# A decoder layer that begins with x: two input blocks first, sums of squares on TensorE, S5 parameters on GpSimd, memory keys and values between the memory-query blocks

## The chip, the cores and the metric

The kernel runs on one core of one Trainium2 chip. The metric is device time in microseconds (us) of one execution. A core has TensorE (PE), which multiplies, VectorE (DVE), ScalarE (ACT) and GpSimd (POOL) for elementwise work, and SyncE (SP), which here issues all large DMAs. Each engine works through its own list of instructions strictly in order, and waits on semaphores for what others produce.

## The reference

One layer of a hybrid decoder trunk, for 512 prompt tokens and 8 sample tokens (520 columns in all). The start of the layer, cut to what the change touches:

```
h = rmsnorm(x, norm1_g)                       # x * rsqrt(mean(x*x) + EPS) * g
u, q, k, v, qm, gl = split(h @ w_in)          # u 512 wide, qm 512, q, k, v 768 each, gates 3072
b_ssm = glu(gelu(s5_scan(u, ...)))            # diagonal complex state space model
#   dt = exp(log_dt); mag = exp(a_re*dt); ab = mag*(cos(a_im*dt) + i sin(a_im*dt)); q = (ab - 1)/a; bb = q*b
#   s = scan over tokens of (ab*s + bb@u);  y = Re(c@s) + d*u
b_att = dilated windowed attention of q, k, v
mk, mv = split(rmsnorm(mem, mem_norm_g) @ w_mem_kv)   # 256 memory tokens
b_mem = softmax(qm @ mk.T) @ mv @ w_mem_o
x = x + (sum of sigmoid(gate_b) * branch_b) @ w_out
x = x + (gelu(conv(h2 @ w_up_a)) * (h2 @ w_up_v)) @ w_down
```

## The kernel before

Weights come in blocks of 128 x 1024 fp32 (512 KB), one SP DMA each (`wload`). For full precision each block is split into a rounded high part (ACT, line 163) and the remainder (DVE, the subtraction at line 80, called from `wload`). A product is three matmuls (lines 192, 193 and 195 in `dense`): high by high, low activations by high weights, high by low. An input block (u0 to u3, qm0 to qm3, k0 to k5, q, v) is 8 row chunks by 2 halves of 260 columns by 3 products, 48 matmuls. `wahead(4)` keeps four blocks loading ahead. Dense results lie in two PSUM slots (`ps_dense`), small ones in four (`ps_small`); block n can begin only when the result of block n-2 has been evacuated.

RMSNorm is applied late: the raw products are multiplied by the reciprocal root of each token at evacuation (`rstd`; `mrs` and `mrt` for the memory). `rms_stat` sums the squares over partitions with a matmul against ones, makes the root by Newton steps on DVE (tiles `xr_*`, `mr_*`), and `rms_bcast` spreads it with diagonal matrices (`xr_dg`) and matmuls into `ps_xb`, copied to `rstd` (line 248).

The program begins with the memory: memT, then keys (mk0 to mk3, 24 matmuls of 256 columns each) and values (mv0 to mv3, 12 matmuls of 512 columns each), then u0 to u3, qm, k, q, v, the gates. The squares of x and memory are made by ACT and added on GpSimd (`xacc`, `macc`).

The S5 branch: `s5_params` (tiles `s5t`, on DVE) makes powers of the decay and a rotation (`rotc`, `rots`) out of a small DMA (line 382), with polynomials in place of exp and sin; `s5_rot` doubles that rotation into tables `rc` (GpSimd) and `rsn` (DVE); `s5_start` opens tables (`gr`, `gi`, `gt`) and four batches (`s5_batches`), which are coroutines fed between the matmuls of the blocks. A scheduler sets each engine's order from emission and priority: `urgent()` raises a piece by PRIO, and `s5_params` is lowered by LOWP; the order is then fixed in the program.

Of the kernel before, what the change touches and what calls it, by code (L numbers as in the profile page):

```python
# [15 lines left out]
OP = mybir.AluOpType  # L16
# [24 lines left out]
POOLW = ("in1",)  # L41
# [5 lines left out]
def order(*names):  # L47
# [3 lines left out]
FIRST = order("u0", "u1", "u2", "u3", "qm0", "qm1", "qm2", "qm3", "k0", "k1", "k2", "k3", "k4", "k5",  # L51
              "q0", "q1", "q2", "q3", "q4", "q5")
# [4 lines left out]
TD0, TD1, TD2, TD3, TD4 = 18, 8, 4, 9, 8  # L57
# [3 lines left out]
def build(nc, tc, I, O):  # L61
# [53 lines left out]
    def weights():  # L115
        for f in range(4):
            yield f"mk{f}", I["wmk"][f]
        for c in range(4):
            yield f"mv{c}", I["wmv"][c]
        for i in [IN0[n] + f for n, f in FIRST] + list(range(20, 26)):  # L120
            yield f"in{i}", I["wi"][i]
# [26 lines left out]

    def wload():
# [68 lines left out]
    def rms_stat_(pt, accs, n, name, pl):  # L218
# [7 lines left out]
        V.tensor_scalar(ms_, pt[:, :nb], 1.0 / D, EPS, OP.mult, OP.add)  # L226
# [63 lines left out]
    mv = mp.tile([P, 2, 512], F32, name="mv")  # L290
    ms_cm, ms = pool("memstage", 1, side="right")
# [39 lines left out]
    def s5_params():  # L331
# [7 lines left out]
        def ts(a, s1, op0, s2=None, op1=None):  # L339
            o = tn(a.shape)  # L340
            if op1 is None:
                V.tensor_scalar(o, a, s1, None, op0)
            else:
                V.tensor_scalar(o, a, s1, s2, op0, op1)
            return o

        def t2(a, b, op):
            o = tn(a.shape)
            tt(V, o, a, b, op)
            return o  # L350
# [118 lines left out]

    def mem_squares():  # L470
        tt(G, macc, memT[:, 0], memT[:, 0], OP.mult)
        for k in range(1, KB):
            msq = ms.tile([P, NMEM], F32, tag=f"xsq{k % 2}", name=f"msq{k}")
            A.activation(msq, memT[:, k], AF.Square)
            tt(G, macc, macc, msq, OP.add)

    def x_part(k):
        S.dma_start(xt[:, k:k + 2], I["xT"][:, k:k + 2])
        for i in (k, k + 1):
            split(xh[:, i], xl[:, i], xt[:, i], gv[:, 0, i:i + 1])  # L480
            if i == 0:
                A.activation(xacc, xt[:, i], AF.Square)
            else:
                sq = ms.tile([P, NT], F32, tag=f"xsq{i % 2}", name=f"xsq{i}")
                A.activation(sq, xt[:, i], AF.Square)
                tt(G, xacc, xacc, sq, OP.add)

    pmk = []
    for f in range(4):
# [1080 lines left out]
```

## Time and profile before

| | |
|---|---|
| median of 3 runs | 988.45 us (987.79 to 993.16) |
| the profiled execution | 990.76 us |
| its span | 989.0 us |
| PE busy | 947.1 us, 96% of the span |
| DVE, ACT, POOL busy | 554.0, 299.6, 192.6 us |

The span is the time between the first and the last recorded instruction; the 1.8 us beside it are start and end of the launch. The profiled execution was 2.3 us above the median. PE is busy nearly everywhere, so the time is what PE has to do plus the places where it stands still or runs at a lower clock.

### The profile page before, as it was taken

The numbers are of one execution on the slowest core, as the hardware profiler recorded it, in microseconds if no ns is written. First come the engines' busy times: TensorE is split into PE (matmuls) and PEld (weight loads), VectorE is DVE, ScalarE is ACT, GpSimd is POOL, SyncE is SP. The second block draws the span as 40 slices with busy tenths as digits, with TensorE's granted clock in tenths as the row PEclk, the third lists the DMA queues.
The fourth block names the chain that finished last, engine by engine and source line by source line (L and its number), as shares of the span: only waits on it lengthen the run. The fifth ranks groups of instructions, "written<-read, shape, count | busy, mean of one in ns | idle before, by whom it ended". The sixth has DMA issues, their size and how long they took to land.

```text
span 989.0 us, 19819 instructions
## 1 busy us (share of the span) xinstructions
PE 947.1 (96%) x8373; PEld 914.1 (92%) x8373; DVE 554.0 (56%) x1017; ACT 299.6 (30%) x480; POOL 192.6 (19%) x261
## 2 busy tenths in 40 slices
PE   8798899989999999999999999999999999999996
PEld 7597899877999998999999999999999999999995
DVE  6999976445455434344655676555555555423234
ACT  6412232224354322123323233322323322222220
POOL 4359542012003301100210350000000000012110
PEclk9998999989999999999999999999999999999998
DMA  7543335531322127563322532223223223332312
GB/s 236 188 152 107 92 104 192 149 95 65 133 87 75 44 68 243 195 229 116 96 91 92 162 118 95 86 93 100 86 86 106 88 85 97 91 99 80 97 39 87
DMA packets 47305, 112.36 MB, mean 114 GB/s; under 512 B 13600, under 2 KB 21408, under 8 KB 45600
## 3 DMA queue, kind: packets, MB, share of 16 engines
q1 hardware_dynamic: 47216, 111.09, 35.0%
q8 instruction: 66, 1.08, 0.4%
q14 instruction: 23, 0.19, 0.1%
HBM read 101.36 MB, written 9.71 MB: 112 GB/s over the span
## 4 chain that ended last, share of the span: by engine, by line
PE 58%; DVE 1%; POOL 1%; ACT 0%; issue 0%; DVEq 0%; ACTq 0%; POOLq 0%
PE ps_y L192 4%; PE ps_y L195 4%; PE ps_y L193 4%; PE ps_uv L195 4%; PE ps_uv L192 4%; PE ps_uv L193 4%; PE ps_ua L192 4%; PE ps_ua L195 4%; PE ps_ua L193 4%; PE ps_g L192 3%; PE ps_g L195 3%; PE ps_g L193 3%; PE ps_x L195 2%; PE ps_x L192 2%; PE ps_x L193 2%; PE ps_me L193 1%
## 5 line engine op out<-in xcount | busy, mean ns | idle before, releaser
L192 PE MATMUL ps_g<-xh,wh_in 128*128 128x260 f32 x384 | 102.0, 287 | 0.0
L193 PE MATMUL ps_g<-xl,wh_in 128*128 128x260 f32 x384 | 99.9, 282 | 0.0
L192 PE MATMUL ps_y<-gh,wh_dn 128*128 128x260 f32 x352 | 93.0, 283 | 0.0
L193 PE MATMUL ps_y<-gl,wh_dn 128*128 128x260 f32 x352 | 93.0, 283 | 0.0
L192 PE MATMUL ps_uv<-hh,wh_uv 128*128 128x260 f32 x352 | 91.9, 282 | 0.0
L192 PE MATMUL ps_ua<-hh,wh_ua 128*128 128x260 f32 x352 | 91.8, 282 | 0.0
L193 PE MATMUL ps_uv<-hl,wh_uv 128*128 128x260 f32 x352 | 91.6, 282 | 0.0
L193 PE MATMUL ps_ua<-hl,wh_ua 128*128 128x260 f32 x352 | 91.6, 282 | 0.0
L163 ACT CAST wh_in<-wr_in 128x1024 fp32r<-128x1024 f32 x50 | 52.3, 1051 | 106.4 <-PE ps_g L193 35.8
L195 PE MATMUL ps_g<-xh,wl_in 128*128 128x260 f32 x384 | 77.2, 283 | 0.0
L192 PEld LDWEIGHTS ps_g<-xh,wh_in 128*128 128x128 f32 x384 | 72.3, 188 | 2.6 <-issue 2.4
L195 PE MATMUL ps_y<-gh,wl_dn 128*128 128x260 f32 x352 | 74.4, 282 | 0.0
L80 DVE TENSOR_TENSOR wl_in<-wr_in,wh_in 128x1024 fp32r<-128x1024 f32 x49 | 67.5, 1378 | 8.8 <-ACT wh_in L163 7.2
L193 PEld LDWEIGHTS ps_g<-xl,wh_in 128*128 128x128 f32 x384 | 72.2, 188 | 0.0
L195 PE MATMUL ps_uv<-hh,wl_uv 128*128 128x260 f32 x352 | 71.2, 283 | 0.0
L195 PE MATMUL ps_ua<-hh,wl_ua 128*128 128x260 f32 x352 | 70.9, 283 | 0.0
L192 PEld LDWEIGHTS ps_uv<-hh,wh_uv 128*128 128x128 f32 x352 | 66.4, 189 | 0.0
L192 PEld LDWEIGHTS ps_ua<-hh,wh_ua 128*128 128x128 f32 x352 | 66.3, 188 | 0.0
L193 PEld LDWEIGHTS ps_y<-gl,wh_dn 128*128 128x128 f32 x352 | 66.2, 188 | 0.0
L192 PEld LDWEIGHTS ps_y<-gh,wh_dn 128*128 128x128 f32 x352 | 66.2, 188 | 0.0
L193 PEld LDWEIGHTS ps_uv<-hl,wh_uv 128*128 128x128 f32 x352 | 66.1, 188 | 0.0
L193 PEld LDWEIGHTS ps_ua<-hl,wh_ua 128*128 128x128 f32 x352 | 66.1, 188 | 0.0
(440 smaller groups left out, 2497.5 us busy)
## 6 DMA issues: line engine op xcount, KB each, us to landing
wr_in<-in_wi SPq DMA_DIRECT2D x50, 512.0 KB, 3.4
wr_ua<-in_wup SPq DMA_DIRECT2D x22, 512.0 KB, 3.3
wr_uv<-in_wup SPq DMA_DIRECT2D x22, 512.0 KB, 3.3
wr_dn<-in_wdn SPq DMA_DIRECT2D x16, 448.0 KB, 3.3
wr_glu<-in_wglu SPq DMA_DIRECT2D x8, 512.0 KB, 3.2
mkc<-in_smk SPq DMA_DIRECT2D x4, 1024.0 KB, 6.4
mvc<-in_smv SPq DMA_DIRECT2D x4, 1024.0 KB, 6.2
wr_out<-in_wout SPq DMA_DIRECT2D x8, 512.0 KB, 3.2
```

The source lines that it names most:

```text
L80: e.tensor_tensor(o, a, b, op)
L163: A.copy(hi[:, a:b], raw[:, a:b])
L192: T.matmul(ps[:, a:b], lhsT=wh, rhs=ah[:, t0:t1], start=st, stop=False)
L193: T.matmul(ps[:, a:b], lhsT=wh, rhs=al[:, t0:t1], start=False, stop=False)
L195: T.matmul(ps[:, a:b], lhsT=wl, rhs=ah[:, t0:t1], start=False, stop=en)
```

## The change

- x and the input blocks u0 and u1 are loaded first, in pieces (`wload_begin`, `x_part`), and u0 and u1 are computed together, chunk by chunk. Their raw products are copied by ACT to `spare[1]` (storage of kT that is not in use yet). Memory follows.
- The sums of squares are made on PE: ACT writes the squares to `spare`, and matmuls with 32 columns of ones add them (`square_sums`), 16 for x, 8 for the memory; `rms_stat` divides by 32 copies.
- `s5_params` runs on GpSimd. What was one scalar-tensor-tensor instruction on DVE becomes a TENSOR_SCALAR and a TENSOR_TENSOR (`t3`, `horner`). `s5_rot` and `s5_decay` are emitted right behind the evacuations of u, with temporaries in kT.
- The memory blocks go between the qm blocks: mk0, mk1 after qm1, mk2, mk3 after qm2, mv0 to mv3 after qm3. `s5_start` comes after mv3.
- `s5_batches` sends the state part of batch n+1 ahead of the output part of batch n, with `ug`, `fr`, `fi` in two buffers.

The diff at its core ("..." marks what is left out):

```diff
-FIRST = order("u0", "u1", "u2", "u3", "qm0", "qm1", "qm2", "qm3", "k0", "k1", "k2", "k3", "k4", "k5",
-              "q0", "q1", "q2", "q3", "q4", "q5")
+FIRST = order("u0", "u1", "u2", "u3", "qm0", "qm1", "mk0", "mk1", "qm2", "mk2", "mk3", "qm3", "mv0", "mv1", "mv2",
+              "mv3", "k0", "k1", "k2", "k3", "k4", "k5", "q0", "q1", "q2", "q3", "q4", "q5")
...
+    def wload_begin(name, src):
+        raw = wp.tile([P, 1024], F32, tag="wr", name=f"wr_{name}", bufs=WB[0])
+        hi = wp.tile([P, 1024], F32R, tag="wh", name=f"wh_{name}", bufs=WB[1])
+        lo = wp.tile([P, 1024], F32R, tag="wl", name=f"wl_{name}", bufs=WB[1])
+        wfly.append((name, hi, lo))
+
+        def part(a, b):
+            S.dma_start(raw[:, a:b], src[:, a:b])
+            A.copy(hi[:, a:b], raw[:, a:b])
+            tt(V, lo[:, a:b], raw[:, a:b], f32(hi[:, a:b]), OP.subtract)
+        return part
...
-    def rms_stat_(pt, accs, n, name, pl):
+    def rms_stat_(pt, accs, n, name, pl, copies=1):
...
-        V.tensor_scalar(ms_, pt[:, :nb], 1.0 / D, EPS, OP.mult, OP.add)
+        V.tensor_scalar(ms_, pt[:, :nb], 1.0 / (copies * D), EPS, OP.mult, OP.add)
...
-        def t3(a, s, b, op0, op1):
-            o = tn(a.shape)
-            stt(o, a, s, b, op0, op1)
+        def t3(a, s, b, op0, op1, o=None):
+            o = tn(a.shape) if o is None else o
+            G.tensor_scalar(o, a, s, None, op0)
+            tt(G, o, o, b, op1)
             return o
 
         def horner(x, cs):
             o = tn(x.shape)
-            V.tensor_scalar(o, x, float(cs[0]), None, OP.mult)
+            G.tensor_scalar(o, x, float(cs[0]), None, OP.mult)
             for c in cs[1:]:
-                stt(o, o, float(c), x, OP.add, OP.mult)
+                t3(o, float(c), x, OP.add, OP.mult, o)
             return o
...
-        V.tensor_copy(rotc, cth[:, 16:112])
-        V.tensor_copy(rots, sth[:, 16:112])
+        G.tensor_copy(rotc, cth[:, 16:112])
+        G.tensor_copy(rots, sth[:, 16:112])
...
+    def square_sums(ps, sqs, n, first):
+        for j, sq in enumerate(sqs):
+            for p, t0, t1 in ps:
+                T.matmul(p[32 * j:32 * j + 32, 0:t1 - t0], lhsT=ones[:, 0:32], rhs=sq[:, t0:t1], start=first,
+                         stop=not first, skip_group_check=True)
+
+    def x_square(k):
+        sq = spare[k // 5][:, NT * (k % 5):NT * (k % 5 + 1)]
+        A.activation(sq, xt[:, k], AF.Square)
+        return sq
+
+    def x_part(k):
+        S.dma_start(xt[:, k], I["xT"][:, k])
+        split(xh[:, k], xl[:, k], xt[:, k], gv[:, 0, k:k + 1])
...
+    w0, w1 = (wload_begin(*next(wsrc)) for _ in range(2))
+    w0(0, 512)
+    x_part(0)
+    w1(0, 512)
+    for k in (1, 2, 3):
+        x_part(k)
+    w0(512, 1024)
+    w1(512, 1024)
+    for k in (4, 5, 6, 7):
+        x_part(k)
     S.dma_start(ident, I["ident"])
+    xsq = [x_square(k) for k in range(KB)]
...
+        with urgent():
+            tt(V, mkT[:, f], ps[:, :NMEM], mrs, OP.mult)
+        if f == 3:
+            S.dma_start(O["mkT"], mkT)
...
-                a, b, c, d = (b5.tile(n, F32, tag=f"tx{j}0", name=f"rt{i}{g0}{j}") for j in range(4))
+                a, b, c, d = (spare[1][:, 256 * j:256 * j + (g1 - g0) * m].rearrange("p (g m) -> p g m", m=m)
+                              for j in range(4))
...
-            if fb == 0:
-                s5_rot()
-                s5_decay()
-            yield 0, TD0 if fb == 0 else TD1
+            yield 0, TD1
...
+            state = fb, ug, *s5_state(fb, ug)
+            yield 1, 0
+            if sent is not None:
+                yield from s5_out(*sent)
+            sent = state
+        yield 0, BD0
+        yield from s5_out(*sent)
...
+    ps01 = [ps_dense(f"ps_u{f}") for f in range(2)]
+    w01 = [wget(f"in{f}") for f in range(2)]
+    for k in range(KB):
+        for f in range(2):
+            dense(ps01[f], w01[f], k, xacts[k:k + 1], first=(k == 0), last=(k == KB - 1))
+    wahead(2)
+    raw01 = []
+    for f in range(2):
+        r = spare[1][:, (3 + f) * NT:(4 + f) * NT]
+        A.copy(r, ps01[f][:, ALL])
+        raw01.append(r)
+    wahead(AHEAD)
+    psq = [ps_small(f"ps_xq{h}") for h in range(2)]
+    for i in (0, 4):
+        square_sums([(psq[h], *HALVES[h][2:]) for h in range(2)], xsq[i:i + 4], NT, i == 0)
+    for k in range(0, KB, 2):
+        mem_part(k)
+    S.dma_start(cri, I["s5c"][:, 0:2])
+    S.dma_start(sdd, I["s5d"])
+    S.dma_start(s0, I["s5s"])
     with urgent():
-        for b in range(2):
-            A.activation(mv[:, b], pmv[:, b * 512:(b + 1) * 512], AF.Identity, scale=mrt[:, b:b + 1])
-    S.dma_start(O["mv"], mv)
-    ptx = ps_small("ps_xr")
-    xrt = rms_stat(ptx, [xacc], NT, "xr", ms)
-    ps0 = dense_in(IN0[FIRST[0][0]] + FIRST[0][1], "".join(map(str, FIRST[0])))
+        for h in range(2):
+            A.copy(xacc[:, HN * h:HN * h + HN], psq[h][:, 0:HN])
+    u2 = dense_in(2, "u2")
+    xrt = rms_stat(ps_small("ps_xr"), [xacc], NT, "xr", ms, 32)
+    u3 = dense_in(3, "u3")
     rms_bcast([ps_small("ps_xb0"), ps_small("ps_xb1")], xrt, NT, rstd, "xr", ms)
-    close(ms_cm)
-    zz = zp.tile([P, KB, NT], F32R, tag="zx", name="zz")
-    zh, zl = zz[:, 0:4], zz[:, 4:8]
-    ut_cm, utp = pool("ut", 1, side="right")
-    ut = utp.tile([P, 8, 80], F32, name="ut")
-    G.memset(ut, 0.0)
+    for f in range(2):
+        evac_u(f, raw01[f], 0)
+    evac_u(2, u2)
+    evac_u(3, u3)
+    mrs = ms.tile([P, NMEM], F32, name="mrs")
+    msq = [mem_square(k) for k in range(KB)]
+    s5_rot()
+    s5_decay()
...
+    mrt = None
+    for n, f in FIRST[4:]:
+        if n == "mk":
+            if f == 0:
+                rms_bcast([ps_small("ps_mb")], mrt, NMEM, mrs, "mr", ms)
+            mem_k(f)
+            continue
+        if n == "mv":
+            mem_v(f)
+            if f == 3:
+                close(ms_cm)
+                zz = zp.tile([P, KB, NT], F32R, tag="zx", name="zz")
+                zh, zl = zz[:, 0:4], zz[:, 4:8]
+                s5t.append(side.add(s5_start(), SD))
+            continue
+        ps = dense_in(IN0[n] + f, f"{n}{f}")
+        if n == "qm":
             evac_qk(qm[:, f], qms[:, f], ps, False)
+            if f == 0:
+                pmq = ps_small("ps_mq")
+                for i in (0, 4):
+                    square_sums([(pmq, 0, NMEM)], msq[i:i + 4], NMEM, i == 0)
+                A.copy(macc, pmq[:, 0:NMEM])
+                mrt = rms_stat(ps_small("ps_mr"), [macc], NMEM, "mr", ms, 32)
```

What the change does to the order, at three places. First DVE, where u is evacuated and the rotation begins. The names: `xr_dg` are the diagonal matrices that spread the roots of x, `ps_u` the products of u, `rotc` and `rots` the rotation out of `s5_params`. Before, a run of DVE's list; all five `xr_dg` and the copies to `rstd` stand ahead of it:

```order
L80 TENSOR_TENSOR ut<-ps_u_699,rstd 128x64x8
L80 TENSOR_TENSOR ut<-ps_u_699,rstd 128x8 x2
L83 SCALAR_TENSOR_TENSOR s5t_279<-s5t_279,s5t_268 128x112
L80 TENSOR_TENSOR s5t_291<-s5t_277 128x112
L83 SCALAR_TENSOR_TENSOR s5t_279<-s5t_279,s5t_268 128x112
L344 TENSOR_SCALAR s5t_293<-s5t_291 128x112
L342 TENSOR_SCALAR s5t_287<-s5t_279 128x112
L80 TENSOR_TENSOR pwr<-s5t_245,s5t_293 128x16
L450 COPY rotc<-s5t_293 128x96
L83 SCALAR_TENSOR_TENSOR s5t_289<-s5t_277,s5t_287 128x112
L556 COPY rc<-rotc 128x16
```

In the change, a run of the same engine that ends with the first of the five `xr_dg` (`kT` holds the temporaries of `s5_rot`, `meml` is the memory's low part, `wl_in_535` the low weights of qm0):

```order
L568 COPY rc<-rotc 128x16
L569 COPY rsn<-rots 128x16
L82 SCALAR_TENSOR_TENSOR xr_ri<-xr_rq,xr_ri 128x5
L79 TENSOR_TENSOR kT<-rc,rots 128x16
L79 TENSOR_TENSOR wl_in_535<-wr_in_533,wh_in_534 128x1024
L79 TENSOR_TENSOR xr_rq<-xr_ri 128x5
L82 SCALAR_TENSOR_TENSOR meml<-memT,gv,memh 128x256
L82 SCALAR_TENSOR_TENSOR xr_rq<-xr_rq,xr_ms 128x5
L79 TENSOR_TENSOR wl_in_541<-wr_in_539,wh_in_540 128x1024
L82 SCALAR_TENSOR_TENSOR xr_ri<-xr_rq,xr_ri 128x5
L79 TENSOR_TENSOR kT<-rsn,rotc 128x16
L248 TENSOR_SCALAR xr_dg_720<-ident,xr_ri 128x128
```

What moved: the first use of `rotc` stood behind the evacuation of the first u block, and stands ahead of the last Newton steps and of every `xr_dg` in the change; it reads what GpSimd writes there.

Second, DVE further on, where the evacuation of u2 and u3 from PSUM (`ps_u_588`, `ps_u_663`) stands in the change, and the rows ahead of it:

```order
L79 TENSOR_TENSOR rsn<-kT 128x8x32
L82 SCALAR_TENSOR_TENSOR mr_rq<-mr_rq,mr_ms 128x2
L82 SCALAR_TENSOR_TENSOR mr_ri<-mr_rq,mr_ri 128x2
L79 TENSOR_TENSOR mr_rq<-mr_ri 128x2
L82 SCALAR_TENSOR_TENSOR mr_rq<-mr_rq,mr_ms 128x2
L82 SCALAR_TENSOR_TENSOR mr_ri<-mr_rq,mr_ri 128x2
L248 TENSOR_SCALAR mr_dg_958<-ident,mr_ri 128x128
L248 TENSOR_SCALAR mr_dg_961<-ident,mr_ri 128x128
L254 COPY mrs<-ps_mb 128x256
L79 TENSOR_TENSOR ut<-ps_u_588,rstd 128x64x8
L79 TENSOR_TENSOR ut<-ps_u_588,rstd 128x8 x2
L79 TENSOR_TENSOR ut<-ps_u_663,rstd 128x64x8
```

The last doublings of the rotation (`rc`, which GpSimd writes) and the whole root of the memory (`mr_*`) stand ahead of these evacuations; before, each u block was evacuated as it ended, and the doublings began behind the last of them.

Third, GpSimd in the change, from the DMA'd parameters on (`s5t_203`), the beginning of a chain that ends in `rc`:

```order
L353 TENSOR_SCALAR s5t_207<-s5t_203 128x16
L79 TENSOR_TENSOR s5t_384<-s5t_203 128x16
L79 TENSOR_TENSOR s5t_386<-s5t_203 128x16
L353 TENSOR_SCALAR s5t_209<-s5t_207 128x16
L79 TENSOR_TENSOR s5t_388<-s5t_384,s5t_386 128x16
L351 TENSOR_SCALAR s5t_211<-s5t_209 128x16
L363 TENSOR_SCALAR s5t_213<-s5t_211 128x16
L363 TENSOR_SCALAR s5t_216<-s5t_211 128x16
L79 TENSOR_TENSOR s5t_213<-s5t_213,s5t_207 128x16
```

and further on in the same list, its end:

```order
L79 TENSOR_TENSOR kT<-rsn,rots 128x128
L79 TENSOR_TENSOR rc<-kT 128x16x8
L79 TENSOR_TENSOR kT<-rc,rotc 128x256
L79 TENSOR_TENSOR kT<-rsn,rots 128x256
L79 TENSOR_TENSOR rc<-kT 128x16x16
L79 TENSOR_TENSOR kT<-rc,rotc 128x256
L79 TENSOR_TENSOR kT<-rsn,rots 128x256
L79 TENSOR_TENSOR rc<-kT 128x8x32
```

Before, GpSimd's list held the additions of squares here, and the first of its `rc` rows stood behind the first tables:

```order
L80 TENSOR_TENSOR t_0_799<-bbi,rwi 128x512
L80 TENSOR_TENSOR t_0_799<-bbi,rwr 128x512
L80 TENSOR_TENSOR t_0_800<-cri,pwi 128x576
L80 TENSOR_TENSOR t_0_801<-cri,pwr 128x576
L80 TENSOR_TENSOR rt_818<-rc,rotc 128x16
L80 TENSOR_TENSOR rt_819<-rsn,rots 128x16
L80 TENSOR_TENSOR t_1_1182<-bbi,rwi 128x512
L80 TENSOR_TENSOR rc<-rt_818,rt_819 128x16
```

## Rows read from the trace of the kernel before

**Rows 1.** Head of the page, and busy time of each engine

```profile
span 989.0 us, 19819 instructions
...
PE 947.1 (96%) x8373; PEld 914.1 (92%) x8373; DVE 554.0 (56%) x1017; ACT 299.6 (30%) x480; POOL 192.6 (19%) x261
```

**Rows 2.** Windows: us; PE, PEld, DVE, ACT, POOL busy; PEclk; DMA; GB/s

```profile
27.28:46.50 19.22, 15.02 (x61) 11.27 (x62) 19.10 (x50) 7.34 (x11) 7.13 (x5) 0.92 0.50 165
...
73.00:81.39 8.39, 4.27 (x27) 3.69 (x27) 8.18 (x12) 1.59 (x4) 7.24 (x7) 0.81 0.49 141
```

**Rows 3.** PE, timeline: start us, us, instruction, idle before and releaser

```profile
79.00 1.12 PE L616 MATMUL ps_gt<-ident,gr 128*128 128x128 f32 x4 [3.58 <-DVE gr L80]
...
81.39 0.57 PE L192 MATMUL ps_qm<-xh,wh_in 128*128 128x260 f32 x1
```

**Rows 4.** Windows behind the start

```profile
100.00:130.00 30.00, 26.32 (x310) 24.20 (x310) 22.28 (x40) 5.68 (x11) 13.61 (x17) 0.94 0.28 74
...
172.00:184.00 12.00, 10.39 (x123) 8.95 (x123) 7.47 (x15) 2.79 (x6) 1.68 (x3) 0.86 0.32 84
...
208.00:220.00 12.00, 8.73 (x109) 7.00 (x108) 6.81 (x11) 2.05 (x5) 1.47 (x2) 0.72 0.49 159
```

**Rows 5.** PE, timeline of the memory blocks

```profile
13.62 0.28 PE L494 MATMUL ps_mk<-memh,wh_mk 128*128 128x256 f32 x1
...
16.46 0.28 PE L494 MATMUL ps_mk<-memh,wh_mk 128*128 128x256 f32 x1
...
33.19 0.39 PE L519 MATMUL ps_mv<-wh_mv,memh 128*128 128x512 f32 x1
...
33.42 0.39 PE L520 MATMUL ps_mv<-wl_mv,memh 128*128 128x512 f32 x1
```

**Rows 6.** Windows of the first DMAs

```profile
0.00:5.00 5.00, 3.94 (x18) 3.95 (x19) 0.26 (x5) 1.47 (x2) 0.74 (x6) 1.00 0.48 86
...
5.00:10.00 5.00, 2.94 (x11) 2.06 (x10) 3.48 (x7) 4.18 (x11) 1.47 (x2) 1.00 0.88 337
```

**Rows 7.** SP and DVE, timeline at the S5 parameters

```profile
9.98 0.43 SPq L382 DMA_DIRECT2D s5t<-in_s5p  x1
...
12.91 0.40 DVE L344 TENSOR_SCALAR s5t<-s5t 128x16 f32<-128x16 f32 x1 [0.22 <-DMA s5t<-in_s5p]
```

**Rows 8.** POOL's groups by form: busy us, mean ns of one, idle before

```profile
L80 POOL TENSOR_TENSOR bbr<-s5t,s5t 128x256 f32<-128x256 f32 x1 | 0.7, 742 | 0.0
...
L80 POOL TENSOR_TENSOR tz<-tz 128x128 f32<-128x128 f32 x2 | 1.0, 488 | 0.2
...
L962 POOL TENSOR_SCALAR p<-p,fn 128x256 f32<-128x256 f32 x12 | 5.6, 479 | 0.0
...
L80 POOL TENSOR_TENSOR rt<-rc,rotc 128x16 f32<-128x16 f32 x1 | 0.7, 672 | 0.0
...
L80 POOL TENSOR_TENSOR rc<-rt,rt 128x16 f32<-128x16 f32 x1 | 1.2, 1207 | 0.0
```

**Rows 9.** POOL, timeline

```profile
93.67 0.33 POOL L80 TENSOR_TENSOR rc<-rt,rt 128x64 f32<-128x64 f32 x1
94.07 0.94 POOL L80 TENSOR_TENSOR rt<-rc,rotc 128x128 f32<-128x128 f32 x1
...
139.80 0.25 POOL L80 TENSOR_TENSOR sn<-vr,tz 128x32 f32<-128x32 f32 x1
140.01 0.43 POOL L80 TENSOR_TENSOR sn<-vi,tz 128x32 f32<-128x32 f32 x1
...
624.24 0.19 POOL L1297 COPY co<-a 128x2 f32<-128x2 f32 x1 [8.22 <-DVE a L80]
624.36 0.46 POOL L1298 COPY co<-a 128x8 f32<-128x8 f32 x1
```

**Rows 10.** DVE, timeline

```profile
83.93 1.04 DVE L80 TENSOR_TENSOR ut<-ps_u,rstd 128x512 f32<-128x512 f32 x1
```

**Rows 11.** Windows of tile s5t alone: us, DVE, POOL busy, PEclk, DMA, GB/s

```profile
0.00:81.39 81.39, 23.95 (x116) 3.88 (x6) 0.96 0.58 189
```

More of the change, by code (lines that the diff above doesn't have):

```diff
@@ L115, in weights @@
     def weights():
[L116 to L120, printed above, removed]
+        for n, f in FIRST:
+            yield (f"{n}{f}", I["wm" + n[1]][f]) if n in ("mk", "mv") else (f"in{IN0[n] + f}", I["wi"][IN0[n] + f])
+        for i in range(20, 26):
             yield f"in{i}", I["wi"][i]
@@ L477, in x_part @@
-    def x_part(k):
-        S.dma_start(xt[:, k:k + 2], I["xT"][:, k:k + 2])
-        for i in (k, k + 1):
[L480 to L489, printed above, removed]
+    prio[0] = PRIO
@@ L645, in s5_batches @@
                 yield 0, 1
-            pr = slice(4 * fb, 4 * fb + 4)
-            e1, e2, gt, tm = tabs[fb]
-            ug = bt([P, 8, 80], "ug", fb)
+            ug = bt([P, 8, 80], "ug", fb, 2)
             S.dma_start(ug, du[fb].rearrange("i (c g) x -> (i c) (g x)", g=8))
             yield 0, 4
-            pvv = [ps_small(f"ps_v{fb}{j}") for j in range(2)]
-            for lp in range(4):
-                for j in range(2):
-                    for g2 in range(2):
-                        T.matmul(pvv[j][64 * g2:64 * g2 + 64, lp * 72:(lp + 1) * 72],
-                                 lhsT=gt[j][:, lp * P + 64 * g2:lp * P + 64 * g2 + 64],
-                                 rhs=ug[:, 2 * lp + g2, 8:80], start=True, stop=True)
@@ L695, in s5_batches @@
-            yield 1, BD0
-            zg = bt([P, 8, 72], "zg", fb)
-            py = [ps_small(f"ps_y{fb}{h}") for h in range(2)]
-            for lp in range(4):
-                cols = slice(lp * 72, (lp + 1) * 72)
-                for h in range(2):
-                    g = 2 * lp + h
-                    for m in range(0, P, 64):
-                        T.matmul(py[h][m:m + 64, cols], lhsT=tm[:, g, m:m + 64], rhs=ug[:, g, 0:72],
-                                 start=True, stop=False, skip_group_check=True)
-                for e, f, last in ((e1, fr, False), (e2, fi, True)):
-                    for m in range(0, P, 64):
-                        for h in range(2):
-                            rows = slice(64 * h, 64 * h + 64)
-                            T.matmul(py[h][m:m + 64, cols], lhsT=e[rows, lp, 1:9].rearrange(fl)[:, m:m + 64],
-                                     rhs=f[rows, lp, 0:72], start=False, stop=last, skip_group_check=True)
-                if lp < 3:
-                    yield 0.7, BD1
@@ new lines, in s5_out @@
+    def s5_out(fb, ug, fr, fi):
+        e1, e2, gt, tm = tabs[fb]
+        zg = bt([P, 8, 72], "zg", fb)
+        py = [ps_small(f"ps_y{fb}{h}") for h in range(2)]
+        for lp in range(4):
+            cols = slice(lp * 72, (lp + 1) * 72)
+            for h in range(2):
+                g = 2 * lp + h
+                for m in range(0, P, 64):
+                    T.matmul(py[h][m:m + 64, cols], lhsT=tm[:, g, m:m + 64], rhs=ug[:, g, 0:72],
+                             start=True, stop=False, skip_group_check=True)
+            for e, f, last in ((e1, fr, False), (e2, fi, True)):
+                for m in range(0, P, 64):
+                    for h in range(2):
+                        rows = slice(64 * h, 64 * h + 64)
+                        T.matmul(py[h][m:m + 64, cols], lhsT=e[rows, lp, 1:9].rearrange(fl)[:, m:m + 64],
+                                 rhs=f[rows, lp, 0:72], start=False, stop=last, skip_group_check=True)
+            if lp < 3:
+                yield 0.7, BD1
+        for h in range(2):
+            A.activation(zg.rearrange("p (l h) x -> p h l x", h=2)[:, h],
+                         py[h][:, :288].rearrange("p (l x) -> p l x", l=4), AF.Gelu_apprx_tanh)
+        s5done["bat"] = fb + 1
+        s5t.append(side.add(s5_z(fb, zg), 5))
+        yield 0.7, 0
```

229 lines of the change are left out of this document (105 added, 124 removed).

## The prediction

> **What bounds the kernel now.** I read the page's head first: PE is busy 947.1 us of a span of 989.0, so 42 us is all that PE stands idle, and any change must either shorten those gaps or push work into them [rows 1]. I then cut the start into windows. Between 27 and 46 us DVE is busy 19.10 of 19.22 us while PE waits for it; between 73 and 81 us PE is busy 4.27 of 8.39 at a granted clock of 0.81 [rows 2]. The wait in that second window is for `gr` of the S5 tables, 3.58 us in one piece; at 81.39 PE takes up qm0 again [rows 3], of which 18 of 48 matmuls stand ahead of these transposes in PE's list. Behind that point three windows lose time: 100 to 130 has 3.7 us idle and 6% of 30 us in clock (5.5 us lost), 172 to 184 has 1.6 idle and 14% of 12 (3.3), 208 to 220 has 3.3 idle and 28% of 12 (6.6) [rows 4]. PE's list has the transposes and outputs of the S5 batches there, so I put these losses down to waits for scans and tables. So 15.4 us is what a perfect overlap of batches could return there. Everything before 81.39 is a start whose length is decided by DVE, DMA and the order of blocks.
>
> I measure the change at one point: the moment at which qm0 starts and runs through, and the work still left for PE then.
>
> **Work left at that point.** Before, at 81.39, the memory blocks were done. In the change PE does mk0 to mk3 and mv0 to mv3 after qm0 starts, apart from 12 matmuls of mk0 that its list has ahead. A key block goes from 13.62 to 16.46, 2.84 us for 24 matmuls; a value matmul has a pitch of 0.23 [rows 5]. So keys are 4 x 2.84 less 12 x 0.118, 9.9 us; values 48 x 0.23, 11.0. The 18 matmuls of qm0 done before are 2.1 more (0.118 each), and eight S5 transposes done before about 1.0 (an estimate: four took 1.12 at the low clock [rows 3], eight at the full clock about as long). Together 24.0 us. Weights do not limit this: 512 KB in 2.84 us is 185 GB/s, and the first DMAs ran at 337 [rows 6].
>
> **When qm0 starts.** The order shows who gates it. qm0 needs the PSUM slot of u2, which DVE frees in four rows that stand behind the whole root of the memory and behind the last doublings of `s5_rot`. Those read `rc` of GpSimd, whose list runs from the first parameter operation to that `rc` in 178 instructions, nearly all one dependent chain. PE cannot escape: the `xr_dg` behind DVE's copy of `rotc` already hold it in the middle of u3. What is queued behind that copy on DVE is the root of x, the low weights of qm0 and qm1, and all evacuations; behind those, PE.
>
> Start of the chain: some 3.2 MB (x, u0, u1) are ahead of the small parameter DMA. The first 10 us moved 5 x 86 + 5 x 337 KB per us, 2.1 MB [rows 6]; the other 1.1 MB at 337 takes 3.2, so about 13 us. Before, issue at 9.98 was followed by use at 12.91 [rows 7]; the change has 14 issues ahead at about 0.45 each, and if small packets overtake, the lower bound is 10.
>
> Prices on GpSimd. Counted by width, the 178 are 100 of at most 32 columns, 17 of 64, 43 of 96 or 112, 9 of 128, 9 of 256. At 256 columns one takes 0.742, at 128 0.488, a TENSOR_SCALAR of 256 0.479 [rows 8]. At 64 the next dependent one begins 0.40 after the start; at 32 a free one begins 0.21 after [rows 9]. Adding the 0.07 that the dependent pair shows between end and start, I take 0.80, 0.52 and 0.38 for 256, 128 and 64, and 0.40 for 112, the middle between both kinds. At 32 and below no undisturbed dependent row exists; 0.25 of duration is the nearest, I take 0.26. Sum: 26.0 + 6.5 + 17.2 + 4.7 + 7.2 = 61.6 us. Bounds: with 0.21, 0.33, 0.33, 0.45 and 0.70 it is 51; with 0.40 for the narrow ones, 0.5 up to 112, 0.94 and 1.0 above, as rows beside a busy DVE have it [rows 8, 9], 88. Hand-overs within the chain wait for DVE while it copies `rstd`, evacuates u0 (1.04 for the wide part [rows 10]) and makes a low weight: 4 us, 2 to 6. So the last `rc` needed comes at 13 + 61.6 + 4 = 79. Behind it DVE has the last products, half a Newton root of some ten tiny operations, two diagonal matrices, a trip over PE, and the evacuations of 1.04 each: 8 us, 6 to 10. **qm0 starts at 87**, 5.6 later than 81.4; with all low ends at 69, and 105 where a third of the upper prices holds.
>
> **A rule on these prices.** The row of the S5 tiles has 23.95 us on DVE in 116 instructions [rows 11]. The Trainium skill, "GPSIMD Engine Reference", section "Performance versus the Vector engine", gives 1.96 times for a wide elementwise operation on GpSimd, and advises DVE for these. By it the parameter part would be an estimated 47 us against about 51 of my sum without the rotation, and the total 1006. No row here compares one narrow operation on both engines undisturbed. The rule speaks against this part of the change, as the rows do.
>
> **What costs nothing.** The 24 square matmuls (about 0.12 each, 2.9 us in all), the interleaving of u0 and u1, the raw copies and squares on ACT, and the removal of GpSimd's square sums all lie before 79 us. u0 to u3 are 192 matmuls, 23 us; with x in at 13 PE is through by about 40 even with the squares, and then stands for GpSimd. If that cover were gone (a chain of under 25 us), the squares would cost 2.9. The freed DVE time at the start buys nothing, since DVE waits for the same chain.
>
> **What the batch overlap returns.** Up to 15.4 us, down to none. The order has new stops: the state transposes of the last table sit behind DVE's scans of the batch before, and the last output parts follow one another with no dense matmul between. Each such stop in before cost 3 to 6 us with its clock [rows 4]; I set one large and one small against the gain, 15.4 - 7.4, **8 us gained** (0 to 15).
>
> **Sum.** +5.6 + 24.0 - 8 = +21.6. On the profiled execution (990.76: span 989.0 and 1.8 around it) 1012.4; that execution was 2.3 above the median of 988.45, so **1010 us**.
>
> **Rivals.**
> - *GpSimd is quick on narrow operations.* Two small copies began 0.12 apart [rows 9]. With 0.12, 0.20, 0.25, 0.35 and 0.60 the chain is 35 us, qm0 starts at 13 + 35 + 2 + 8 = 58, and the time is 988.45 - 23.4 + 24.0 - 8 = 981, faster. For it: those rows were neighbours without dependence. Against: the chain is dependent. It decides below a chain of about 38 us; from there to 48 the change is within 0.5% of nothing.
> - *GpSimd beside DVE is slower than I took.* 16-column operations that ran beside a busy DVE took 0.67 and 1.21 [rows 8]. If 40 of the 100 narrow ones fall beside DVE's splits of x, weights and memory at 0.4 more, that is 16 to 18 us: qm0 at 105, 1028. Against: DVE itself waits for most of the chain. The skill's "SBUF — State Buffer", section "SBUF: two separate sides", has a lock between the two engines that stops one of them for the other's whole instruction; these two rows agree with it.
> - *The overlap gives all 15.4.* Then 1003. Against: the new stops in the order.
> - *The chain is not the gate*, since PE reaches qm0 without it: then qm0 starts at about 45 and the time falls to 968. Against: the slot of u2 is freed only by rows that the order puts behind it. I give this almost nothing.
>
> **Numbers.** My forecast with its own bounds (994 to 1022, which holds the third rival too): 0.58. Slow GpSimd beyond 1022: 0.14. Within 0.5% of 988.45 (983.5 to 993.4; about what a measurement of this kernel can tell from no change): 0.13. Quick GpSimd, faster than 983.5: 0.15, the last rival in it. So faster 0.15, same 0.13, slower 0.72. The range 981 to 1027 leaves out about 0.12 below and 0.08 above.
>
> **What would show it.** GpSimd busy almost without a gap from 13 to near 79; DVE's copy of `rotc` waiting for GpSimd some 35 us; PE idle in the middle of u3 from about 32; qm0's first matmul at about 87, after a wait put down to DVE's evacuation of u2; memory keys and values of 21 us behind it; fewer or shorter stops of PE in the 100 us after. I am wrong if GpSimd's narrow operations follow one another at under 0.18, or if PE enters qm0 before 65.

## The result, and the profile after

The change made the kernel slower: 1027.49 us median of 4 runs (1026.8 to 1032.43) against 988.57 of the kernel before, a ratio of 1.0394 with a 95% interval of 1.0349 to 1.044. The prediction was slower at 1010 us with a range of 981 to 1027, so the direction held, and so did most of the mechanism at the start; the gain forecast behind it did not come, and the time came out half a microsecond beyond the range.

The head of the page of the changed kernel, to be read beside [rows 1]:

```profile
span 1025.3 us, 19930 instructions
...
PE 947.8 (92%) x8421; PEld 914.4 (89%) x8421; DVE 529.3 (52%) x899; ACT 302.1 (29%) x486; POOL 211.6 (21%) x398
```

PE's busy time is the same to within 0.7 us. The other 35.6 of the 36.3 us by which the span is longer are time in which PE does nothing.

What PE waited for, in us in total, times, and the longest:

```profile
PE ps_xb L251 <- DVE xr_dg L248: 25.2, 2, 18.4
PE ps_mb L251 <- DVE mr_dg L248: 15.1, 1, 15.1
PE ps_u L201 <- DVE wl_in L79: 4.9, 1, 4.9
PE ps_gt L626 <- DVE gr L79: 4.2, 1, 4.2
```

The first two are DVE's diagonal matrices, for the root of x and that of the memory. Together 40 us, and neither of them is long work on DVE. What DVE waited for stands in its timeline; the bracket at the end is the idle time before the instruction and its releaser:

```profile
26.83 0.18 DVE L386 TENSOR_SCALAR s5t<-s5t 128x32 int32<-128x32 f32 x1 [10.11 <-POOL s5t L351]
...
53.42 0.41 DVE L568 COPY rc<-rotc 128x16 f32<-128x16 f32 x1 [18.20 <-POOL rotc L460]
...
65.60 0.22 DVE L79 TENSOR_TENSOR kT<-rc,rots 128x32 f32<-128x32 f32 x1 [7.70 <-POOL rc L79]
...
75.06 0.23 DVE L79 TENSOR_TENSOR kT<-rc,rots 128x64 f32<-128x64 f32 x1 [7.83 <-POOL rc L79]
...
82.37 1.63 DVE L79 TENSOR_TENSOR wl_mk<-wr_mk,wh_mk 128x1024 fp32r<-128x1024 f32 x1
83.92 0.15 DVE L232 TENSOR_SCALAR mr_ms<-ps_mr 128x2 f32<-128x2 f32 x1
...
87.26 0.67 DVE L82 SCALAR_TENSOR_TENSOR mr_ri<-mr_rq,mr_ri 128x2 f32<-128x2 f32 x1
...
89.78 0.16 DVE L82 SCALAR_TENSOR_TENSOR mr_ri<-mr_rq,mr_ri 128x2 f32<-128x2 f32 x1
...
92.57 1.03 DVE L79 TENSOR_TENSOR ut<-ps_u,rstd 128x512 f32<-128x512 f32 x1
```

DVE's copy of `rotc` stood 18.2 us behind GpSimd, two further products of the rotation 7.7 and 7.8, and a conversion ahead of them 10.1. The Newton steps of the memory's root (`mr_ri`, at 87.26 and 89.78) took 0.67 beside GpSimd and 0.16 alone. u2 is evacuated from 92.57 on. GpSimd's own list, at the first parameters, at a run of narrow operations of which each needs the one before, at operations of 112 columns, at `rotc`, at two pairs of 16 columns beside DVE's low weights, and at the `rc` that the last doublings need:

```profile
13.51 0.61 POOL L353 TENSOR_SCALAR s5t<-s5t 128x16 f32<-128x16 f32 x1 [11.49 <-DMA s5t<-in_s5p]
14.20 1.21 POOL L79 TENSOR_TENSOR s5t<-s5t 128x16 f32<-128x16 f32 x2
...
18.05 0.26 POOL L363 TENSOR_SCALAR s5t<-s5t 128x16 f32<-128x16 f32 x1
18.39 0.22 POOL L79 TENSOR_TENSOR s5t<-s5t,s5t 128x16 f32<-128x16 f32 x1
18.70 0.25 POOL L363 TENSOR_SCALAR s5t<-s5t 128x16 f32<-128x16 f32 x1
...
36.73 1.43 POOL L363 TENSOR_SCALAR s5t<-s5t 128x112 f32<-128x112 f32 x3
...
53.12 0.26 POOL L460 COPY rotc<-s5t 128x96 f32<-128x96 f32 x1
...
54.24 1.43 POOL L79 TENSOR_TENSOR s5t<-pwi,s5t 128x16 f32<-128x16 f32 x2
...
55.98 1.46 POOL L79 TENSOR_TENSOR s5t<-s5t,s5t 128x16 f32<-128x16 f32 x2
...
81.38 0.78 POOL L79 TENSOR_TENSOR rc<-kT 128x256 f32<-128x256 f32 x1
```

Its windows (PE, PEld, DVE, ACT, POOL busy, PEclk, DMA share, GB/s) over this stretch, and those of tile s5t alone (DVE, POOL busy), which answer to [rows 11]:

```profile
13.50:82.20 68.70, 31.71 (x227) 29.11 (x226) 21.66 (x57) 17.01 (x33) 60.86 (x178) 0.70 0.24 77
```

```profile
13.50:82.20 68.70, 0.51 (x3) 51.77 (x153) 0.70 0.24 77
```

GpSimd is busy 60.86 of 68.7 us in exactly the 178 instructions that the prediction counted. On PE, qm0 starts at 94.55 (the last row here, to set beside the last of [rows 3]). The wait that ended last before it is the one for `mr_dg`; between the two rows PE does twelve matmuls of mk0 and does not wait again:

```profile
91.00 1.19 PE L251 MATMUL ps_mb<-mr_dg,ones 128*128 128x128 f32 x4 [15.15 <-DVE mr_dg L248]
...
94.55 0.42 PE L198 MATMUL ps_qm<-xh,wh_in 128*128 128x260 f32 x1
```

Behind it, the windows that lose time in the changed kernel, to be set beside [rows 4]:

```profile
150.00:160.00 10.00, 8.33 (x90) 7.55 (x89) 10.00 (x14) 2.36 (x4) 4.83 (x5) 1.00 0.16 55
...
220.00:240.00 20.00, 15.82 (x254) 14.21 (x254) 14.29 (x23) 4.90 (x13) 7.53 (x8) 0.91 0.30 84
...
250.00:260.00 10.00, 7.56 (x121) 6.13 (x120) 4.95 (x8) 3.17 (x6) 0.00 (x0) 1.00 0.74 227
...
270.00:290.00 20.00, 15.13 (x69) 10.36 (x69) 10.00 (x22) 9.57 (x29) 5.93 (x11) 0.83 0.19 66
```

To compare kernels I added up what PE lost in each window of 10 us: its idle time, and its busy time multiplied by one minus the granted clock. Up to 100 us and from there to 350:

| kernel | lost up to 100 | lost 100 to 350 | median of its runs |
|---|---|---|---|
| before | 21.3 | 18.0 | 988.6 to 990.3 |
| the change | 56.5 | 17.9 | 1027.5 |
| r1 rotation in the tables | 17.6 | 33.0 | 1001.8 |
| r2 parameters on DVE | 14.0 | 18.1 | 986.2 |
| r3 batches of before | 58.3 | 23.0 | 1037.6 |
| r4 before, overlap alone | 23.4 | 10.0 | 982.2 |
| r5 memory behind u | 58.6 | 3.4 | 1012.8 |
| r6 as r5, parameters on DVE | 16.0 | 1.3 | 969.2 |
| r7 as r5, rotation in the tables | 26.4 | 9.4 | 992.7 |
| r8 before, parameters on GpSimd alone | 66.1 | 26.6 | 1039.7 |
| r9 as r6, memory's root later | 16.6 | 1.4 | 969.2 |

So the change lost 35 us at the start and, in sum, gained nothing behind it. The prediction had 30 lost at the start and 8 gained behind.

### The profile page after: what moved, and what is told of

Same layout as the page of the kernel before. It is cut to its first block, busy times and chain, and to the rows that moved or that the text cites. A ratio compares the mean times of both kernels' runs of the same rounds, so it can differ in the third digit from the quotient of the medians.

```text
span 1025.3 us, 19930 instructions
## 1 busy us (share of the span) xinstructions
PE 947.8 (92%) x8421; PEld 914.4 (89%) x8421; DVE 529.3 (52%) x899; ACT 302.1 (29%) x486; POOL 211.6 (21%) x398
## 4 chain that ended last, share of the span: by engine, by line
PE 67%; DMA 2%; DVE 2%; POOL 2%; ACT 1%; issue 1%; DVEq 0%; SPq 0%; ACTq 0%; POOLq 0%
PE ps_y L198 4%; PE ps_g L198 4%; PE ps_y L201 4%; PE ps_uv L201 4%; PE ps_y L199 4%; PE ps_uv L198 4%; PE ps_uv L199 4%; PE ps_ua L198 4%; PE ps_ua L201 4%; PE ps_ua L199 4%; PE ps_g L199 4%; PE ps_g L201 4%; PE ps_x L201 2%; PE ps_x L198 1%; PE ps_x L199 1%; DMA wr_in<-in_wi 1%
## 5 line engine op out<-in xcount | busy, mean ns | idle before, releaser
L79 DVE TENSOR_TENSOR wl_in<-wr_in,wh_in 128x1024 fp32r<-128x1024 f32 (+1 forms) x52 | 66.6, 1284 | 21.3 <-ACT wh_in L169 15.5
L199 PEld LDWEIGHTS ps_uv<-hl,wh_uv 128*128 128x128 f32 x352 | 66.1, 188 | 0.0
L199 PEld LDWEIGHTS ps_ua<-hl,wh_ua 128*128 128x128 f32 x352 | 66.1, 188 | 0.0
```

What stands on the lines that cost most here:

```text
L79: e.tensor_tensor(o, a, b, op)
L199: T.matmul(ps[:, a:b], lhsT=wh, rhs=al[:, t0:t1], start=False, stop=False)
```

## The experiments

The theory: GpSimd's chain of parameters costs through what stands behind its consumers in DVE's list (the roots, the evacuations of u), and so stops PE. The rivals: the new order of blocks is what costs; or the overlap of batches does. The experiments undo one part each.

**r1: the rotation back in the tables' coroutine.** No evacuation stands behind GpSimd's rotation any more; the parameters stay on GpSimd.

```diff
     def s5_rot():
-        V.tensor_copy(rc[:, :, 0:1], rotc[:, 0:16].unsqueeze(2))
-        V.tensor_copy(rsn[:, :, 0:1], rots[:, 0:16].unsqueeze(2))
+        G.tensor_copy(rc[:, :, 0:1], rotc[:, 0:16].unsqueeze(2))
+        G.tensor_copy(rsn[:, :, 0:1], rots[:, 0:16].unsqueeze(2))
...
-                a, b, c, d = (spare[1][:, 256 * j:256 * j + (g1 - g0) * m].rearrange("p (g m) -> p g m", m=m)
-                              for j in range(4))
+                a, b, c, d = (b5.tile(n, F32, tag=f"tx{j}0", name=f"rt{i}{g0}{j}") for j in range(4))
...
-            yield 0, TD1
+            if fb == 0:
+                s5_rot()
+                s5_decay()
+            yield 0, TD0 if fb == 0 else TD1
...
```

> The changed kernel, but the doubling of the rotation stands in the tables' coroutine as before (temporaries from the batch pool, which opens behind the memory blocks), and the two copies that begin it are GpSimd's. The parameters stay on GpSimd. If GpSimd's chain gates the evacuation of u2 only through DVE's order (my theory), qm0 starts at about 50 us in place of 94.6, and the time falls by about 44 to 983 (972 to 992). If the order of the blocks is what costs (memory behind qm, S5 tables late), the start moves but the time stays at 1010 or above.

Measured: 1001.8 us, ratio 1.0118 (1.0087 to 1.0149) to before. The start did what the theory says, less fast than expected: qm0 at 58.3 in place of 94.55 (the first row), and the loss up to 100 us fell from 56.5 to 17.6. But 15 of the 39 us came back behind it. The first S5 transpose is at 123.1 (the second row), 65 us behind qm0, and the rotation, whose temporaries come from the batch pool again, stands there among the tables' first products:

```profile
58.29 0.39 PE L198 MATMUL ps_qm<-xh,wh_in 128*128 128x260 f32 x1
...
123.08 0.27 PE L628 MATMUL ps_gt<-ident,gr 128*128 128x128 f32 x1
```

The later stretch, where the last batches stand (columns as above):

```profile
190.00:270.00 80.00, 62.35 (x603) 51.36 (x600) 40.99 (x77) 24.66 (x68) 20.41 (x30) 0.85 0.33 96
```

Neither theory nor rival foresaw this: my number left out that the S5 stage starts later against the dense blocks. r7, the same edit with the memory blocks ahead of qm0, bears this out: its loss behind 100 us is 9.4 where r1 has 33.0.

**r2: the parameters on DVE, fused as before.** Everything else as in the change.

```diff
         def t2(a, b, op):
             o = tn(a.shape)
-            tt(G, o, a, b, op)
+            tt(V, o, a, b, op)
             return o
 
-        def t3(a, s, b, op0, op1, o=None):
-            o = tn(a.shape) if o is None else o
-            G.tensor_scalar(o, a, s, None, op0)
-            tt(G, o, o, b, op1)
+        def t3(a, s, b, op0, op1):
+            o = tn(a.shape)
+            stt(o, a, s, b, op0, op1)
             return o
...
```

> The changed kernel with the parameters on DVE, fused as before; the rotation stays where the change put it. By the theory of the chain, 24 us of DVE work in place of some 55 us on GpSimd, interleaved with DVE's other rows: qm0 at about 65 us, time about 997 (985 to 1008). If GpSimd's price is not the cause: 1020 or above.

Measured: 986.17 us, ratio 0.9963 (0.9948 to 0.9978), 41 us below the change and a little below before. One part of the change, undone, takes away its whole loss. qm0 starts at 48.92, earlier than the 65 expected, held up by 2 us only:

```profile
48.92 0.39 PE L198 MATMUL ps_qm<-xh,wh_in 128*128 128x260 f32 x1 [1.98 <-DVE ut L79]
```

The loss behind 100 us stays at 18.1, so this part touches the start alone.

**r3 and r4: the overlap of batches, taken out of the change and put alone into the kernel before.** r3 has the `s5_batches` of before, r4 the new one; the core of the edit in r4:

```diff
     def s5_batches():
+        sent = None
         for fb in range(4):
...
+            state = fb, ug, *s5_state(fb, ug)
+            yield 1, 0
+            if sent is not None:
+                yield from s5_out(*sent)
+            sent = state
+        yield 0, BD0
+        yield from s5_out(*sent)
...
```

> The changed kernel with the batches of before (no overlap). By the windows of both traces the overlap returned about 2 us net, so 1027 to 1031. By the prediction's term of 8 us: 1035. If the overlap itself costs: 1022 or below.

> The kernel before with nothing but the overlapped batches. About 2 us returned: 985 to 988. By the prediction's term: 980. By its third rival, all of 15.4: 973. If the overlap makes new stops that outweigh: 992 or above.

Measured: r3 1037.56 us (1.0481, 1.0445 to 1.0516), 10 above the change; r4 982.15 us (0.993, 0.991 to 0.9949), 7 below before. Both say that the overlap is worth 7 to 10 us by the medians (8.0 and 5.1 in the column behind 100 us), as the prediction's term had it, and that my reading before these runs (2 us, because the change lost as much behind 100 as before) was wrong. In r4 the window of 172 to 184, which lost 3.3 us in [rows 4], loses none:

```profile
100.00:130.00 30.00, 26.22 (x318) 24.46 (x317) 24.74 (x43) 6.57 (x13) 18.04 (x22) 0.94 0.35 91
...
172.00:184.00 12.00, 12.00 (x124) 11.86 (x126) 9.92 (x17) 5.14 (x11) 0.43 (x1) 1.00 0.67 208
...
200.00:220.00 20.00, 18.42 (x233) 16.39 (x229) 9.11 (x16) 4.38 (x10) 3.84 (x6) 0.91 0.40 125
```

In r3 the last batches stand alone:

```profile
250.00:290.00 40.00, 29.70 (x259) 24.90 (x258) 16.63 (x32) 13.11 (x30) 6.56 (x13) 0.90 0.39 118
```

So in the change something else takes back what the overlap gives. That is the next question.

**r5: the memory blocks directly behind u3.** The chain on GpSimd stays; only the order of blocks is undone, so that S5 starts with all of qm, k and q still to come.

```diff
-FIRST = order("u0", "u1", "u2", "u3", "qm0", "qm1", "mk0", "mk1", "qm2", "mk2", "mk3", "qm3", "mv0", "mv1", "mv2",
-              "mv3", "k0", "k1", "k2", "k3", "k4", "k5", "q0", "q1", "q2", "q3", "q4", "q5")
+FIRST = order("u0", "u1", "u2", "u3", "mk0", "mk1", "mk2", "mk3", "mv0", "mv1", "mv2", "mv3", "qm0", "qm1", "qm2", "qm3",
+              "k0", "k1", "k2", "k3", "k4", "k5", "q0", "q1", "q2", "q3", "q4", "q5")
...
             if f == 0:
+                pmq = ps_small("ps_mq")
+                for i in (0, 4):
+                    square_sums([(pmq, 0, NMEM)], msq[i:i + 4], NMEM, i == 0)
+                A.copy(macc, pmq[:, 0:NMEM])
+                mrt = rms_stat(ps_small("ps_mr"), [macc], NMEM, "mr", ms, 32)
                 rms_bcast([ps_small("ps_mb")], mrt, NMEM, mrs, "mr", ms)
...
```

> The changed kernel with one thing undone: the memory keys and values stand directly behind u3, ahead of qm0, and S5 starts behind them, with all of qm, k and q still to come as cover. GpSimd's chain stays where it is. If 8 us of the loss are the lateness of the S5 stage (fewer dense blocks beside it), the time falls by about 8 to 1019 (1015 to 1022), since the memory matmuls themselves only change places with qm. If lateness costs nothing: 1026 or above. If the place of the memory is the main cost: 1000 or below.

Measured: 1012.81 us (1.0232, 1.0216 to 1.0249), 14.7 below the change: more than the 8 expected. The start lost the same (58.6), the stage behind it 3.4 in place of 17.9. The first transpose comes at 124.44, 8.6 us behind the start of qm0 at 115.8, where the change has it at 147.8, 53 behind qm0. From 120 to 340 us PE is busy 216.58 of 220 at the full clock:

```profile
124.44 0.27 PE L626 MATMUL ps_gt<-ident,gr 128*128 128x128 f32 x1
```

```profile
120.00:340.00 220.00, 216.58 (x2213) 200.47 (x2211) 140.94 (x276) 79.09 (x181) 56.82 (x77) 1.00 0.39 119
```

So the place of the memory costs 14.5 us. Its matmuls are the same in both; what differs is the cover. In the change the last matmul of q starts at 222.7 and the last output matmul of S5 at 255.2, in r5 at 229.9 and 246.0, so S5 runs on alone for 32 us in the one and 16 in the other. That the delay of S5 past the blocks that would have covered its waits is the whole of it is argued from this: no run moved the start of S5 alone.

**r6: both undone.** The edits of r2 and r5 together; x first, squares on TensorE and the overlap stay.

> Both undone: parameters on DVE and memory directly behind u3 (x first, squares on TensorE and the overlap stay). By the two effects together: 986 less 8 for the S5 stage, and less up to 8 for the wait for the evacuation of u2, which the memory matmuls now cover: 970 (964 to 980). If the effects are not additive: 984 or above.

Measured: 969.17 us, ratio 0.9791 (0.9776 to 0.9806): 58 below the change and 21 below before. 41 and 15 were the single effects, 56 in sum, so they add up. This version beats both kernels. Most of what it still loses lies in two stretches where DVE is busy 19.82 of 20 and 27.82 of 30 us:

```profile
30.00:50.00 20.00, 14.74 (x106) 13.44 (x105) 19.82 (x95) 4.17 (x7) 6.72 (x15) 0.83 0.41 122
...
60.00:90.00 30.00, 24.49 (x159) 21.76 (x157) 27.82 (x41) 8.52 (x13) 17.91 (x13) 0.94 0.54 178
```

**r7: as r5, with the rotation as in r1.** The edits of r1 and r5 together.

> Memory directly behind u3, parameters on GpSimd, the rotation in the tables' coroutine as before with its first copies on GpSimd, so that no evacuation stands behind GpSimd's chain. If the parameters on GpSimd cost only through what is queued behind them: 975 to 985, since the tables still wait for the end of a chain of some 60 us. If GpSimd's length itself decides: 995 or above.

Measured: 992.71 us (1.0036, 1.0017 to 1.0055), above the 985 that I gave at most, and 23.5 above r6, which differs in the engine of the parameters and the place of the rotation. PE's longest waits:

```profile
PE ps_qm L198 <- DVE qms L79: 6.6, 1, 6.6
PE ps_u L201 <- DVE wl_in L79: 6.4, 1, 6.4
```

Both are again waits for DVE rows behind others that wait for GpSimd. The low weights of u2 stand behind a conversion to integers of the parameters (the first row). The evacuation of qm0 (94.78) stands behind the table products on DVE, which waited for the end of the parameters and for GpSimd's own table product:

```profile
27.07 0.18 DVE L386 TENSOR_SCALAR s5t<-s5t 128x32 int32<-128x32 f32 x1 [10.10 <-POOL s5t L351]
...
82.01 0.88 DVE L79 TENSOR_TENSOR gr<-bbr,rwr 128x512 f32<-128x512 f32 x1 [3.05 <-POOL pwi L79]
...
86.52 1.58 DVE L79 TENSOR_TENSOR gr<-gr,t 128x512 f32<-128x512 f32 x1 [2.82 <-POOL t L79]
...
94.78 0.68 DVE L79 TENSOR_TENSOR qm<-ps_qm,rstd 128x512 f32<-128x512 f32 x1
```

Lifting one consumer out of DVE's list is not enough as long as others stand in it.

**r8: the kernel before with nothing but the parameters on GpSimd.** The edit is the `s5_params` part of the change's diff.

> The kernel before with nothing but the parameters on GpSimd. DVE's list has the copy of the rotation ahead of the memory's root and of the low parts of the value weights and of x, so by the theory (what is queued on DVE behind a value of GpSimd's chain) DVE stands until about 60 us and the time rises by 20 to 35: 1010 to 1025. If the parameters on GpSimd cost only in the new order of blocks: 995 or below.

Measured: 1039.68 us (1.0516, 1.049 to 1.0541), 50 above before, 15 more than my upper end. The same mechanism in the old order: DVE's copy of the rotation waits for GpSimd, and PE for the value weights that stand behind it on DVE.

```profile
58.02 1.25 DVE L557 COPY rc<-rotc 128x16 f32<-128x16 f32 x1 [23.95 <-POOL rotc L451]
```

```profile
PE ps_mv L521 <- DVE wl_mv L80: 33.1, 2, 23.0
...
PE ps_xr L223 <- POOL xacc L80: 7.9, 1, 7.9
```

The second wait is one that I had not counted: in this order GpSimd also adds the squares of x, which now stand among the chain.

**r9: as r6, with the spread of the memory's root behind mk1.**

```diff
+        pmk.append(ps)
+        if f == 1:
+            rms_bcast([ps_small("ps_mb")], mrt, NMEM, mrs, "mr", ms)
         with urgent():
-            tt(V, mkT[:, f], ps[:, :NMEM], mrs, OP.mult)
+            while f and pmk:
+                tt(V, mkT[:, f + 1 - len(pmk)], pmk.pop(0)[:, :NMEM], mrs, OP.mult)
...
```

> As r6 (parameters on DVE, memory behind u3), with the matmuls that spread the memory's root behind mk1 in place of ahead of mk0, so that PE has two key blocks to do while DVE makes the root. In r6 PE stood 4.4 us at that place. If this wait is on the path: 965 (963 to 967). If DVE sets the pace there anyway: 968 to 970.

Measured: 969.23 us (0.9797, 0.9777 to 0.9817), the same as r6. The wait of 4.4 us is gone, and PE's busy time from 30 to 50 us rises from 14.74 to 19.26; but from 70 to 90 it falls to 9.12 at a clock of 0.66, with DVE busy 19.73 of 20, and the wait for the first transpose, 2.7 us in r6, is 8.3 here, with no releaser named:

```profile
30.00:50.00 20.00, 19.26 (x166) 17.93 (x166) 19.75 (x84) 5.62 (x6) 3.70 (x7) 1.00 0.64 190
...
70.00:90.00 20.00, 9.12 (x64) 8.62 (x68) 19.73 (x28) 3.95 (x9) 13.38 (x8) 0.66 0.34 111
```

```profile
PE ps_gt L630 <- issue: 8.3, 1, 8.3
```

The profiled execution of r9 was 2.8 us above the median of its runs, so the size of this last gap is uncertain. With DVE busy almost throughout both stretches, I read it as DVE setting the pace of that start: a gap of PE filled there opens again 30 us later.

## Why the prediction came out as it did

- **What bounds the start: right in the chain, wrong in the last wait.** That the roots and the evacuations of u stand behind GpSimd's chain in DVE's list, and that `xr_dg` holds PE in the middle of u3, is in the trace row by row, and r2 and r8 show it from both sides: taking the parameters off GpSimd returns 41 us, putting them alone on GpSimd costs 50. But the last wait before qm0 is not for u2's evacuation, as predicted: it is for `mr_dg`, 15.15 us. u2's rows end by 93.7, while PE is still at the twelve matmuls of mk0 that its list has ahead of qm0. DVE's copy of `rotc` waited 18.2 us and not some 35; DVE had stood 10.1 before it, at a conversion ahead of u2's low weights; PE stopped in u3 at 39.3 and not at 32.
- **The rivals.** The one in which GpSimd is quick, and the one in which the chain isn't the gate, are out. The one in which DVE slows GpSimd gave 1028, and 1027.5 came, but not on its way: it had 40 narrow operations slowed and qm0 at 105. In the trace nine of the 100 narrow ones took 0.46 to 1.27 us, all of them while DVE worked, some 5 us in all, and qm0 came at 94.55. That its number fits is luck.
- **The chain: right, 3 us short.** It began at 13.5 (13 predicted) and reached the last `rc` that counts at 82.2 (79), 68.7 us against 61.6 + 4. With DVE idle, narrow operations followed one another at 0.18 when they were independent and at 0.31 to 0.34 when not, around the 0.26 that I took; scalar ones of 112 columns took 0.49 where I had 0.40. The parameter part, tile s5t, is 51.77 us against the 51 of my sum; the Trainium skill, "GPSIMD Engine Reference", section "Performance versus the Vector engine", with its 1.96 times, measured on 2048 columns, would have given an estimated 47. The direction of that page agrees with the trace; here the ratio would be 1.86 on the sum of DVE and POOL time in [rows 11], but with every fused operation split in two.
- **Behind the chain: mis-sized, 8 us predicted, 12.4 measured** (82.2 to 94.55). On DVE the root's matrices were begun at 90.57: the last doublings ran on until 89.7, a low weight of 1.63 that I had not counted stood among them, and the tiny Newton steps in between took 0.57 to 0.68 each beside GpSimd where they take 0.15 alone. u2's rows then ended at 93.7, and the twelve matmuls of mk0 ahead of qm0, at a granted clock of 0.50, kept PE until 94.55.
- **qm0 at 87: measured 94.55**, 7.6 late by these two points.
- **Work left, 24 us: right.** qm0 starts 13.2 later, and behind it the span is 930.75 us long where it was 907.61, 23.1 more; together these are the 36.3 between the profiled executions. Less what PE lost behind qm0 (35.6 and 36.4, added up in windows of 2.5 us), the work itself differs by 23.9.
- **The batches: the step that failed is the sum behind qm0, "8 us gained".** Nothing to speak of was gained (0.8 by the sums of the last point). The overlap itself returns 7 to 10 (r3, r4). What I set against it was two stops inside the new batches. What stood against it was a term that I did not have: the memory blocks were moved ahead of the start of S5, so that its four batches had 12 dense blocks beside them in place of 16 (r5: 14.7 us). A second term that my sum did not have goes the other way: the doubling of the rotation no longer stands among the first tables. r7 has it there and r5 has not, with 9.4 and 3.4 lost behind 100 us. In that column, 18.0 before, less 8.0 for the overlap (r4), less 6.0 for the rotation, and 14.5 more for the place of the memory make 18.5; the change has 17.9.
- **The median.** The prediction took off the 2.3 us by which the profiled execution of before was above the median; that of the change was 0.4 below its own. 2.7 us of the difference are in that. 7.6, 8 and 2.7 make 18.3, against the 17.5 between 1010 and 1027.5; the rest is the 23.1 in place of 24.0.
- **The range.** With qm0 at 94.55 and 8 gained, or with qm0 at 87 and nothing gained, the same sum gives 1018, inside the range; it took both to pass its end. The 105 "where a third of the upper prices holds" does not come out of the prediction's own terms: with a third, and the upper ends of the hand-overs and of the tail, it is 99; half of them would give 104.

So the mechanism of the start was right with another last wait, and the sum was short in two places, the tail of the start and the S5 stage behind it.

What stays open: r7 is 23.5 us above r6, and this was read from its waits alone; what of it belongs to the engine of the parameters and what to the place of the rotation was not told apart. x first and the squares on TensorE were not run alone: r6, which has them with the overlap and the early rotation, is 13 us below r4, which has the overlap alone, and their share of that is not known.

## What to carry to other kernels

An engine that is idle is no free place for a serial chain: before moving one, list what stands behind its consumers in the order of every other engine, since that is where its length is paid. When blocks are reordered, count how many dense blocks are left beside each stage that waits; a stage that starts later loses its cover, and this can eat a gain that was made elsewhere in the same change. Of a change in several parts, run the parts: here three of them (the overlap, the rotation ahead of the tables, and x first with the squares on TensorE) make a kernel of 969 us, and the two others turn it into one of 1027.

## What the runs showed of the hardware

- In the changed kernel a GpSimd operation of 16 columns took 0.20 to 0.26 us while DVE was idle, and the next dependent one began 0.31 to 0.34 after its start; beside DVE's work some took 0.53 to 1.27. Operations of 112 columns mostly took 0.37 to 0.49. Seven times the width cost less than twice the time, so this chain of 178 was priced by its number more than by its widths.
- DVE operations of 2 columns from SBUF took 0.15 us alone and 0.57 to 0.68 while GpSimd worked on 256 columns; the one that read PSUM (`mr_ms`, at 83.92) took 0.15 beside GpSimd too. The Trainium skill, "SBUF — State Buffer", section "SBUF: two separate sides", tells of a lock between the two engines held for a whole instruction; these rows agree with it.
- PE's granted clock was 0.70 on the mean from 13.5 to 82.2 us, with waits of 6.8 to 18.4 us in between. Behind the wait of 15.15 us it was 0.50, the lower of its two levels (1.2 of 2.4 GHz), from 91.0 to 95.6, and qm0's first matmuls took 0.42 in place of 0.28.
